# A streaming encoder layer on one core: attention in five steps, five heads' queries and keys by half products in front, small loads on another queue

## The chip, the cores and the metric

The kernel runs on one core of a Trainium2 chip. The metric is the device time of one execution in microseconds. The kernel before takes 2172.08 us, the median of three runs (2170.55 to 2174.25).

## What is computed

One layer with two parallel branches, for a prompt of 512 tokens and eight decode requests of 16 tokens each, so T = 640 columns in the kernel (NPT = 512 of them prompt). The width is 2048. Cut to what matters here:

```python
z = x @ w_in                      # q, k, v, forget logit and gate of FoX; GatedDeltaNet's inputs; merge gates
s = jnp.einsum('bqhd,bkhd->bhqk', q, k) * FOX_SCALE
bias = c_q - c_k                  # running sums of log forget, per head
p = jax.nn.softmax(jnp.where(visible, s + bias, -jnp.inf), axis=-1)
o_a = jnp.einsum('bhqk,bkhd->bqhd', p, v)
y_a = (o_a * jax.nn.silu(gate_a)) @ w_out_fox
...
h = (jax.nn.sigmoid(m_a) * y_a + jax.nn.sigmoid(m_b) * y_b) @ w_out
x1 = layer_norm(DEEPNORM_ALPHA * x + h, ln_g, ln_b)
x_out = x1 + jax.nn.sigmoid(x1 @ w_pl_gate) * rms_norm(p_l @ w_pl_proj, pl_norm_w)
```

FoX attention has eight heads of width 128. The prompt attends to itself; the decode tokens attend to caches of 512 keys and values per request (`kc`, `vc`) and to themselves.

## The kernel before

The activations lie transposed in SBUF, 128 channels by 640 tokens. A *column* is a projection onto 128 output channels: over 16 blocks of the width, every product is made of three matmuls of the halves of its operands (high by high, low by high, high by low), for two halves of 320 tokens. `column` (L396 and L397 in the rows, in its helper) makes 96 matmuls of 320 columns. `pair` (L474) makes two columns at once by seven half products, 168 matmuls in place of 192. The weights come from DRAM in tiles `wr` of 512 KB, issued by SP, are split into a high part `wh` by ACT (L329) and a low part `wl` by DVE (L335).

The phases follow one another: `front` (first columns, values, gates and the pairs), `phase_fox` (attention between the matmuls of plain columns, then a projection), `phase_gdn` (the other branch), `tail`. The order of the work is set when the program is built: every loop over dense matmuls calls `tick`, which lets *lanes* of generators emit their next piece. A generator yields how many ticks it wants to wait, and a model clock (`clock`, `busy`, `wrote`) keeps it from being resumed before its operands are likely to be there. What comes out is a fixed list of instructions for each engine; at run time only semaphores hold an engine back.

The queries and keys of head 0 and of the heads in `APART` (2, 3, 5, 6) are made by `front`, the latter as pairs, stored in a DRAM buffer `qkd`, and loaded again by SP in `phase_fox`. Heads 1, 4 and 7 get theirs from plain columns inside `phase_fox` (six columns), with three merge columns (`mcol`) beside them.

Attention is driven by `fox_all`. For each head `fox_in` loads what is small: the forget sums spread over the partitions (`nb` for the prompt, `nbd` for decode), the gate `sg`, the values `vn`; it also fills `qpad`, a padded copy of the decode queries, on GpSimd. Then four query blocks i = 0 to 3 go through `fox_step`, a pipeline over the list `flow`: `scores` (matmuls `s<-k,q` L754 for i = 0, `s<-kh,qh` and two more for the others at L388 to L390; three operations on DVE, the exponential on ACT), `softmax2` (a reciprocal and a scaling on DVE, L655 and L656), the transposes with the copy to `pT` (L726, L729), and the weighted sum `s<-pT,vn` (L742), which DVE multiplies by the gate into `og`. Within one call of `fox_step` the order before is: transposes of one block, `softmax2` of a later one, weighted sum of an earlier one; the new block's scores come after the call.

The decode tokens have a generator of their own, `fox_dec`: sixteen matmuls against the cached keys (`s<-kc,qpad`, L773), a softmax over `xd`, four transposes into `ppad` and one into `pn` (L793, L799; ACT's copies L795, L801), the weighted sum with `vc`. `fox_out` stores the head.

Each DMA of SP signals one of eight semaphores in turn (DMAHW0 to 7), and a transfer is issued when the one eight before it has landed; GpSimd's transfers have a set of their own (DMASW).

Of the kernel before, what the change touches and what calls it, by code (L numbers as in the profile page):

```python
# [52 lines left out]
class Kernel:  # L53
# [9 lines left out]
    APART = 2, 3, 5, 6  # L63
    NG = 8
    PAIR0, PAIRS = 6, NG + 2 + FRONT // 2 + len(APART)
    BETWEEN = 3, 6
# [6 lines left out]
    def __init__(self, tc, ins, outs):  # L73
        self.clock, self.busy, self.wrote, self.paced = 0.0, [0.0, 0.0, 0.0], {}, False
        self.tc, self.nc, self.i, self.o = tc, tc.nc, ins, outs
        self.lanes, self.every = [], 2
# [4 lines left out]
    def saw(self, ins):  # L81


        if ins.engine not in ENGINES or not ins.outs or not hasattr(ins.outs[0], "ap"):
            return
# [22 lines left out]
    def watch(self, gen):  # L108
# [7 lines left out]
        return abs(n), t + (0.25 if n > 0 else -1.5)  # L116
# [513 lines left out]
    def load_v(self, h):  # L630

        self.vn[h] = self.zt([P, 5, P], "vn", 2)
        self.nc.sync.dma_start(out=self.vn[h], in_=self.vd[:, :, h * P:(h + 1) * P].rearrange("t p d -> p t d"))

    def load_bias(self, h):
        nb = self.zt([P, T], "nb", 2)
        self.nc.sync.dma_start(out=nb, in_=bcast(self.rd[h], T, P))
        nbd = self.zt([P, NPT], "nbd", 2)
        self.nc.sync.dma_start(out=nbd, in_=bass.AP(self.sfd.tensor, self.sfd[h * 8].offset,
# [3 lines left out]
    def softmax1(self, xs, n):  # L643
# [3 lines left out]
        nm = self.zt([P, 1], "nm", 6)  # L647
        nc.vector.reduce_max(out=nm, in_=xs[:, 0:n], axis=AX.X, negate=True)
        sm = self.zt([P, 1], "sm", 6)
# [9 lines left out]
    def fox_in(self, h, q):  # L659

        nc = self.nc
        if h == 0:
            self.load_bias(0)
        self.sg[h] = self.zt([P, T], "sg", 2)
        nc.sync.dma_start(out=self.sg[h], in_=self.sgf[h])
        self.load_v(h)
        if h == 0:
            for j in range(4):
                self.load_kv(0, "k", j)

# [12 lines left out]

    def fox_all(self):


        flow = [None] * 4
        for h in range(H):
            while h not in self.heads or self.heads[h][2] > self.now or min(self.outdone, self.decdone) < h - 2:
                if any(flow):  # L690
                    self.fox_step(flow)
                yield 2
            q, k, _ = self.heads.pop(h)
            self.fox_in(h, q)
# [23 lines left out]
    def fox_step(self, flow):  # L718

        nc = self.nc  # L720
        spread = weigh = None
        if flow[1]:
            h, i, (xs, _) = flow[1]
# [7 lines left out]
        if flow[0]:  # L731
            h, i, (xs, sm) = flow[0]
# [1741 lines left out]
```

## Time and profile before

| | |
|---|---|
| median of three runs | 2172.08 us |
| the profiled execution | 2173.18 us |
| its span | 2171.3 us |
| granted TensorE clock, mean | 0.999 |
| attention stage, first scores to last weighted sum | 739.53 to 941.35 us |
| plain dense work ahead of it in the same phase, from | 721.92 us |

The span is the time between the first and the last instruction of the profiled execution; 1.9 us lie around it. Every row of the profile has an engine, a line of the kernel, an operation with its tiles (result<-operands), a count and times; a window's row has one group for each engine, busy time and count, then the granted clock, the busy share of the DMA engines and the rate. SPq is SP's queue: its rows are issues of transfers, not the transfers. TensorE's busy time in a row includes overlap, since matmuls are pipelined, so start times say more than durations.

### The profile page before, as it was taken

What the parts mean: (1) busy time and instruction counts of PE and PEld (TensorE: products, weight loads), DVE (VectorE), ACT (ScalarE), POOL (GpSimd) and SP (SyncE); (2) the same over time, 40 slices, a digit from 0 to 9 for tenths busy, and PEclk for the clock granted to TensorE, in tenths of its full rate; (3) what the DMA queues carried; (4) which work ended last, traced back from release to release, by engine and by line L of the source; (5) the groups of instructions that cost most, each with busy time, mean ns of one, the idle gap of its engine ahead of it and who ended that gap; (6) DMA issues with size and microseconds to landing.
All of it is one profiled execution on the core that took longest, in us unless ns stands there. A gap on an engine that the chain in (4) does not pass through costs nothing.

```text
span 2171.3 us, 41951 instructions
## 1 busy us (share of the span) xinstructions
PE 2149.0 (99%) x15438; PEld 2082.3 (96%) x15438; DVE 1566.0 (72%) x3207; ACT 1007.3 (46%) x2213; POOL 401.9 (19%) x596
## 2 busy tenths in 40 slices
PE   9999999999999999999999999999999999999998
PEld 7799999999999998899999999999999999999998
DVE  5877776767776565566478677766757787789987
ACT  4344443443444343353655566655443343354544
POOL 0022233323330101002334333332000000021100
PEclk9999999999999999999999999999999999999999
DMA  6356656666554899869978778878567656673465
GB/s 235 101 184 202 189 182 199 198 199 194 184 180 158 276 325 344 314 199 291 241 179 199 180 188 194 189 182 248 161 229 260 209 171 202 201 276 122 153 227 173
DMA packets 240670, 452.65 MB, mean 208 GB/s; under 512 B 38920, under 2 KB 122504, under 8 KB 240464
## 3 DMA queue, kind: packets, MB, share of 16 engines
q1 hardware_dynamic: 224912, 421.64, 59.5%
q0 software_dynamic: 15552, 28.32, 8.0%
q8 instruction: 122, 2.00, 0.4%
q14 instruction: 84, 0.69, 0.1%
HBM read 353.48 MB, written 96.38 MB: 207 GB/s over the span
## 4 chain that ended last, share of the span: by engine, by line
PE 91%; DVE 3%; DMA 3%; ACT 1%; SPq 0%; issue 0%; POOL 0%; ACTq 0%; DVEq 0%; POOLq 0%
PE g L474 44%; PE g L396 18%; PE g L397 18%; PE g L440 2%; PE s L974 1%; PE s L742 1%; PE s L813 1%; PE s L773 1%; DMA ws138b<-ws 0%; PE s L440 0%; PE s L1168 0%; DMA nb<-rd 0%; DVE sx L1006 0%; DVE sx L1004 0%; PE s L726 0%
## 5 line engine op out<-in xcount | busy, mean ns | idle before, releaser
L329 ACT CAST wh<-wr 128x512 fp32r<-128x512 f32 x624 | 381.2, 619 | 288.7 <-PE g L474 109.5
L335 DVE TENSOR_TENSOR wl<-wr,wh 128x512 fp32r<-128x512 f32 x516 | 358.3, 708 | 183.5 <-ACT wh L329 173.7
L474 PE MATMUL g<-xh,wh 128*128 128x320 f32 (+1 forms) x1296 | 402.9, 311 | 2.7 <-ACT m L1278 1.6
L474 PE MATMUL g<-xl,wh 128*128 128x320 f32 (+1 forms) x1296 | 401.2, 310 | 0.6 <-DVE xl L371 0.6
L474 PE MATMUL g<-xh,wl 128*128 128x320 f32 (+1 forms) x1296 | 401.4, 310 | 0.0
L396 PE MATMUL g<-xh,wh 128*128 128x320 f32 (+1 forms) x960 | 313.0, 326 | 0.7 <-ACT wh L329 0.7
L396 PE MATMUL g<-xh,wl 128*128 128x320 f32 (+1 forms) x960 | 297.1, 309 | 0.8 <-DMA wl<-in_w 0.7
L396 PE MATMUL g<-xl,wh 128*128 128x320 f32 (+1 forms) x960 | 297.2, 310 | 0.4 <-DVE xl L371 0.4
L397 PE MATMUL g<-xh,wh 128*128 128x320 f32 x960 | 297.3, 310 | 0.0
L397 PE MATMUL g<-xl,wh 128*128 128x320 f32 x960 | 297.0, 309 | 0.0
L397 PE MATMUL g<-xh,wl 128*128 128x320 f32 x960 | 296.7, 309 | 0.0
L474 PEld LDWEIGHTS g<-xh,wh 128*128 128x128 f32 x1296 | 243.9, 188 | 4.3 <-ACT m L1278 2.1
L474 PEld LDWEIGHTS g<-xl,wh 128*128 128x128 f32 x1296 | 243.7, 188 | 1.1 <-DVE xl L371 1.1
L474 PEld LDWEIGHTS g<-xh,wl 128*128 128x128 f32 x1296 | 244.1, 188 | 0.0
L474 PE MATMUL g<-t,wh 128*128 128x320 f32 (+1 forms) x1088 | 241.4, 310 | 0.0
L335 DVE TENSOR_TENSOR wl<-sr,wh 128x512 fp32r<-128x512 f32 x200 | 147.9, 759 | 98.6 <-ACT wh L329 97.6
L295 POOL TENSOR_TENSOR ws<-ws 128x171 f32<-128x171 f32 (+2 forms) x152 | 116.7, 768 | 541.5 <-DMA ws<-in_w 535.7
L396 PEld LDWEIGHTS g<-xh,wh 128*128 128x128 f32 x960 | 180.9, 188 | 11.9 <-issue 7.1
L474 PEld LDWEIGHTS g<-t,wh 128*128 128x128 f32 x1088 | 181.9, 188 | 0.6 <-issue 0.3
L396 PEld LDWEIGHTS g<-xh,wl 128*128 128x128 f32 x960 | 180.6, 188 | 1.4 <-DMA wl<-in_w 1.0
L397 PEld LDWEIGHTS g<-xh,wh 128*128 128x128 f32 x960 | 181.0, 189 | 0.9
L396 PEld LDWEIGHTS g<-xl,wh 128*128 128x128 f32 x960 | 180.9, 188 | 1.0 <-DVE xl L371 1.0
(440 smaller groups left out, 4148.8 us busy)
## 6 DMA issues: line engine op xcount, KB each, us to landing
wr<-in_w SPq DMA_DIRECT2D x252, 512.0 KB
wl<-in_w POOLq DMA_DIRECT2D x108, 256.0 KB, 5.8
kc<-in_kc SPq DMA_DIRECT2D x32, 512.0 KB
vc<-in_vc SPq DMA_DIRECT2D x32, 512.0 KB
sr<-in_w SPq DMA_DIRECT2D x25, 512.0 KB
ws<-in_w SPq DMA_DIRECT2D x96, 128.0 KB
sb<-in_w SPq DMA_DIRECT2D x80, 128.0 KB
md<-m SPq DMA_DIRECT2D x32, 320.0 KB
```

Of the source, the lines that this page charges most:

```text
L295: nc.gpsimd.tensor_tensor(out=o, in0=x, in1=y, op=op)
L329: nc.scalar.copy(out=hi, in_=src)
L335: nc.vector.tensor_tensor(out=lo, in0=src, in1=hi.bitcast(F32), op=ALU.subtract)
L396: nc.tensor.matmul(ps[0], whl[w], xhl[o][:, a], start=(first and x == 0), stop=(last and x == 2))
L397: nc.tensor.matmul(ps[1], whl[w], xhl[o][:, b], start=(first and x == 0), stop=(last and x == 2))
L440: nc.tensor.matmul(ps, x[:, sl], w, start=(s == 0 and n == 0), stop=(s == 15 and n == 2))
L474: nc.tensor.matmul(ps, a[:, w], b, start=(k == 0 and n == 0 and not more), stop=(k == last and n == 2), skip_group_check=True)
L742: nc.tensor.matmul(ops[:, 0:P], vn[:, kb, :], pT[:, kb * P:(kb + 1) * P], start=(kb == 0), stop=(kb == i))
L773: nc.tensor.matmul(s1[32 * j:32 * j + 32, :], self.qpad[:, 2 * j + par, :], kc[:, (j % 2) * NPT:(j % 2 + 1) * NPT], start=(par == 0), stop ...
L813: nc.tensor.matmul(od[32 * j:32 * j + 32, 0:P], self.ppad[:, c, 2 * j + par, :], vc[:, o:o + P], start=False, stop=(par == 1 and c == 3), ...
L974: nc.tensor.matmul(pp[:, o:o + 256].rearrange("p (a b) -> p a b", a=2), kq[:, 0, x], kq[:, :, x], start=True, stop=True)
```

## The change

- `APART` becomes 1, 2, 3, 6, 7: five heads in `front` by pairs. Only heads 4 and 5 have plain columns in `phase_fox` (`JOBS`), with the three merge columns; their q and k go through `qkd` too. All heads load q and k by a new function `load_qk`.
- `fox_all` loads q, k, nb, nbd and the four key caches of head 0 first, then q and k of head 1 and the four value caches of head 0; `sg` and `vn` of head 0 come with `fox_in`, behind these. For head 0 SP issues them; for later heads GpSimd issues nb, nbd, sg and vn, and q and k from head 2 on. A head starts when the model clock is 21.5 past the start of the one before (`PACE`); lanes may be resumed at every tick (`every`) and without lead (`lead`); transfers no longer count in the model clock.
- `fox_step` takes the new block as an argument and has a list of five: transposes, weighted sum, the new scores, then `softmax2` of the block before. The score tiles are one per block (`xs0` to `xs3`) instead of three in turn.
- The decode part's transposes move into `fox_dec2`, a lane of its own, with `pn` ahead of the four transposes; `xd` has two buffers.
- `weight_sums` does its thirteenth slice in `front`. The tiles of the projection (`pr`) are loaded inside a merge column. In the evacuation of the projection three tiles come from `kc` at once and three from `vc` later; squares use one `kc` tile and one more tile, `og`.

TensorE has 24 dense matmuls fewer by this, GpSimd issues 40 transfers more, SP fewer.

The diff, without buffer counts, `lead`, the DRAM buffers of `qkd` and the host's ordering of the weights:

```diff
@@ -60,10 +60,11 @@
     FRONT = 32 - 3 - 7
-    APART = 2, 3, 5, 6
     NG = 8
+    APART = 1, 2, 3, 6, 7
     PAIR0, PAIRS = 6, NG + 2 + FRONT // 2 + len(APART)
-    BETWEEN = 3, 6
+    PACE = 21.5
+    JOBS = 4, 5, None, None
     FILL = 0, 0, 1, 0, 1, 0, 1, 4
@@ -81,7 +82,7 @@
-        if ins.engine not in ENGINES or not ins.outs or not hasattr(ins.outs[0], "ap"):
+        if ins.engine not in ENGINES or "DMA" in type(ins).__name__ or not ins.outs or not hasattr(ins.outs[0], "ap"):
             return
@@ -630,13 +631,13 @@
         self.vn[h] = self.zt([P, 5, P], "vn", 2)
-        self.nc.sync.dma_start(out=self.vn[h], in_=self.vd[:, :, h * P:(h + 1) * P].rearrange("t p d -> p t d"))
+        (self.nc.gpsimd if h else self.nc.sync).dma_start(out=self.vn[h], in_=self.vd[:, :, h * P:(h + 1) * P].rearrange("t p d -> p t d"))
...
         nb = self.zt([P, T], "nb", 2)
-        self.nc.sync.dma_start(out=nb, in_=bcast(self.rd[h], T, P))
+        (self.nc.gpsimd if h else self.nc.sync).dma_start(out=nb, in_=bcast(self.rd[h], T, P))
         nbd = self.zt([P, NPT], "nbd", 2)
-        self.nc.sync.dma_start(out=nbd, in_=bass.AP(self.sfd.tensor, self.sfd[h * 8].offset,
+        (self.nc.gpsimd if h else self.nc.sync).dma_start(out=nbd, in_=bass.AP(self.sfd.tensor, self.sfd[h * 8].offset,
                                                     [[NPT, 8], [0, 16], [1, NPT]]))
@@ -659,15 +660,9 @@
         nc = self.nc
-        if h == 0:
-            self.load_bias(0)
         self.sg[h] = self.zt([P, T], "sg", 2)
-        nc.sync.dma_start(out=self.sg[h], in_=self.sgf[h])
+        (nc.gpsimd if h else nc.sync).dma_start(out=self.sg[h], in_=self.sgf[h])
         self.load_v(h)
-        if h == 0:
-            for j in range(4):
-                self.load_kv(0, "k", j)
-
         for par in range(2):
@@ -681,26 +676,35 @@
+    def load_qk(self, h):
+        qk = []
+        for c in range(2):
+            qk.append(self.zt([P, T], "qk"[c], 2))
+            (self.nc.gpsimd if h > 1 else self.nc.sync).dma_start(out=qk[c], in_=self.qkd[h, c])
+        self.heads[h] = *qk, self.clock + (7 if h else 5)
+
     def fox_all(self):
...
-        flow = [None] * 4
+        flow, begun = [None] * 5, 0.0
+        self.load_qk(0)
+        self.load_bias(0)
+        for j in range(4):
+            self.load_kv(0, "k", j)
+        self.load_qk(1)
+        for j in range(4):
+            self.load_kv(0, "v", j)
         for h in range(H):
-            while h not in self.heads or self.heads[h][2] > self.now or min(self.outdone, self.decdone) < h - 2:
+            while h not in self.heads or max(self.heads[h][2], begun + self.PACE) > self.clock or min(self.outdone, self.decdone) < h - 2:
                 if any(flow):
...
             q, k, _ = self.heads.pop(h)
+            begun = self.clock
             self.fox_in(h, q)
-            if h == 0:
-                yield 5
-                for j in range(4):
-                    self.load_kv(0, "v", j)
-                yield 4
             parts = None
             for i in range(4):
-                self.fox_step(flow)
-                flow[0] = h, i, self.scores(h, i, q, k, parts)
+                self.fox_step(flow, (h, i, q, k, parts))
                 if i == 0:
@@ -708,19 +712,21 @@
                 if i == 1 and h + 1 < H:
-                    while self.qkdone[1] < h - 1:
+                    while self.qkdone[1] < h - 1 or h + 1 not in self.kept:
                         yield 1
                     self.load_bias(h + 1)
+                    if h:
+                        self.load_qk(h + 1)
         while any(flow):
...
-    def fox_step(self, flow):
-
-        nc = self.nc
-        spread = weigh = None
-        if flow[1]:
-            h, i, (xs, _) = flow[1]
+    def fox_step(self, flow, new=None):
+
+        nc = self.nc
+        spread = ops = None
+        if flow[2]:
+            h, i, (xs, _) = flow[2]
             pt = self.sps()
@@ -728,22 +734,23 @@
             spread = h, i, pT
-        if flow[0]:
-            h, i, (xs, sm) = flow[0]
-            self.softmax2(xs, P * (i + 1), sm)
-            weigh = flow[0]
-        if flow[2]:
-            h, i, pT = flow[2]
-            if i == 0:
-                self.og = self.zt([P, T], "og", 2)
-            vn, sl = self.vn[h], slice(i * P, (i + 1) * P)
+        if flow[3]:
+            h, i, pT = flow[3]
+            vn = self.vn[h]
             ops = self.sps()
...
                 nc.tensor.matmul(ops[:, 0:P], vn[:, kb, :], pT[:, kb * P:(kb + 1) * P], start=(kb == 0), stop=(kb == i))
+            if i == 0:
+                self.og = self.zt([P, T], "og", 2)
+            sl = slice(i * P, (i + 1) * P)
             nc.vector.tensor_tensor(out=self.og[:, sl], in0=ops[:, 0:P], in1=self.sg[h][:, sl], op=ALU.mult)
...
                 self.outs["gens"].append(self.fox_out(h, self.sg[h], self.og))
-        flow[:] = None, weigh, spread, None
+        new = (*new[0:2], self.scores(*new)) if new else None
+        if flow[1]:
+            h, i, (xs, sm) = flow[1]
+            self.softmax2(xs, P * (i + 1), sm)
+        flow[:] = None, new, flow[1], spread, None
@@ -788,6 +795,14 @@
         yield -2
+        self.decs2["gens"].append(self.fox_dec2(h, xd))
+
+    def fox_dec2(self, h, xd):
+        nc = self.nc
+        pt = self.sps()
+        nc.tensor.transpose(pt[:, 0:P], xd[:, NPT:T], self.ident)
+        pn = self.zt([P, P], "sq", 2, "pn")
+        nc.scalar.copy(out=pn, in_=pt[:, 0:P])
         pt = self.dps()
@@ -795,11 +810,7 @@
                 in_=pt.rearrange("p (c j two x) -> p c j two x", c=4, two=2, x=16)[:, :, :, par, :])
-        pt = self.sps()
-        nc.tensor.transpose(pt[:, 0:P], xd[:, NPT:T], self.ident)
-        pn = self.zt([P, P], "sq", 2, "pn")
-        nc.scalar.copy(out=pn, in_=pt[:, 0:P])
-        yield 4
+        yield 2
         while self.outdone < h - 1:
@@ -1506,48 +1517,40 @@
         self.outdone = self.decdone = -1
-        self.heads, self.sg = {}, {}
+        self.heads, self.sg, self.kept = {}, {}, {0, *self.APART}
+        self.every, self.lead = 1, 0.0
         work["gens"].append(self.fox_all())
...
         self.vn = {}
-        ws = self.zt([P, 1024], "ws")
-        self.sums["gens"].append(self.weight_sums([ws[:, x:x + 256] for x in range(0, 1024, 256)], slice(12, 13),
-                                                  (9, 7, 5, 20)))
-        for h in range(H):
-            qk = []
-            if h in self.BETWEEN:
+        todo = deque((h, c) for h in self.JOBS for c in range(1 if h is None else 2))
+
+        def job():
+            h, c = todo.popleft()
+            if h is None:
                 self.mcol("eacc")
-            for c in range(2):
-                stored = (h, c) in self.qkd
-                if not stored:
-                    acc = self.column()[0]
-                self.until(lambda: min(self.qkdone) >= h - 2)
-                x = self.zt([P, T], "qk"[c], 2)
-                qk.append(x)
-                if stored:
-                    nc.sync.dma_start(out=x, in_=self.qkd[h, c])
-                    continue
-                for hf in range(2):
-                    sl = slice(hf * HALF, (hf + 1) * HALF)
-                    if c == 0:
-                        nc.scalar.mul(x[:, sl], acc[hf], FOX_SCALE)
-                    else:
-                        nc.scalar.copy(out=x[:, sl], in_=acc[hf])
-                if c:
-                    nc.sync.dma_start(out=self.o["fk"][h], in_=x)
-            self.heads[h] = *qk, self.now + (9 if stored else 1)
-        for _ in range(2 - len(self.BETWEEN)):
-            self.mcol("eacc")
+                return
+            acc = self.column()[0]
+            x = self.zt([P, T], "pr", 1, "qk")
+            for hf in range(2):
+                sl = slice(hf * HALF, (hf + 1) * HALF)
+                if c == 0:
+                    nc.scalar.mul(x[:, sl], acc[hf], FOX_SCALE)
+                else:
+                    nc.scalar.copy(out=x[:, sl], in_=acc[hf])
+            nc.sync.dma_start(out=self.qkd[h, c], in_=x)
+            if c:
+                nc.sync.dma_start(out=self.o["fk"][h], in_=x)
+                self.kept.add(h)
+        while todo:
+            job()
         op, pr = [], []
-        for k in range(2):
-            if k == 0:
-                self.until(lambda: not self.sums["gens"])
-            pr.append(self.zt([P, 1024], "ws", 1, "pr")[:, 0:T] if k == 0 else self.zt([P, T], "pr"))
-            nc.sync.dma_start(out=pr[k], in_=self.i["pT"][k])
-
         def after(s):
+            if s in (4, 6):
+                self.until(lambda: min(self.qkdone) >= 6)
+                pr.append(self.zt([P, T], "nb", 2, "pr") if s == 4 else self.zt([P, T], "pr"))
+                nc.sync.dma_start(out=pr[-1], in_=self.i["pT"][s // 2 - 2])
             if s in (12, 14):
@@ -1778,11 +1782,14 @@
-            self.until(lambda: self.decdone == 7 and not self.sums["gens"])
+            self.until(lambda: self.qkdone[1] == 7 and not self.sums["gens"])
             self.eacc = self.zt([P, T], "eacc")
-            tiles = [self.zt([P, 1024], *x, "e")[:, 0:T] for x in (("kc", 4), ("kc", 4), ("ws", 1), *[("vc", 4)] * 4)]
-            self.e_tiles, self.q_tiles = tiles[0:5], tiles[5:7]
+            tiles = [self.zt([P, 1024], "kc", 4, "e")[:, 0:T] for _ in range(4)]
+            self.e_tiles, self.q_tiles = tiles[0:3], [tiles[3], self.zt([P, T], "og", 2, "e")]
             self.esq = None
+        if n == 6:
+            self.until(lambda: self.decdone == 7)
+            self.e_tiles += [self.zt([P, 1024], "vc", 4, "e")[:, 0:T] for _ in range(3)]
         e = self.e_tiles[n % len(self.e_tiles)]
```

How the instructions move is shown at three places. The first is SP at the start of attention, behind the stores of the last pair; the names are those of the text above, and the brackets hold the semaphores waited for. Before:

```order
L269 DMA wr<-in_w 128x1024
L269 DMA wr<-in_w 128x1024 [waits DVE_49]
L637 DMA nb<-rd 128x640 [waits DMAHW4_49]
L639 DMA nbd<-sfd 128x1x512
L665 DMA sg<-sgf_169 128x640
L633 DMA vn<-vd 128x5x128
L627 DMA kc<-in_kc 128x1024 [waits DMAHW0_49]
L627 DMA kc<-in_kc 128x1024 [waits DMAHW1_49]
L627 DMA kc<-in_kc 128x1024 [waits DMAHW2_49]
L627 DMA kc<-in_kc 128x1024 [waits DMAHW3_49]
L269 DMA wr<-in_w 128x1024 [waits DMAHW4_49,DVE_49]
L627 DMA vc<-in_vc 128x1024 [waits DMAHW5_49]
```

After:

```order
L628 DMA kc<-in_kc 128x1024 [waits DMAHW3_49]
L628 DMA kc<-in_kc 128x1024 x3
L683 DMA q<-qkd_187 128x640 [waits DMAHW7_49]
L683 DMA k<-qkd_188 128x640 [waits DMAHW0_49]
L628 DMA vc<-in_vc 128x1024 [waits DMAHW1_49]
L628 DMA vc<-in_vc 128x1024 [waits DMAHW2_49]
L628 DMA vc<-in_vc 128x1024 [waits DMAHW3_49]
L628 DMA vc<-in_vc 128x1024 [waits DMAHW4_49]
L270 DMA wr<-in_w 128x1024 [waits DMAHW5_49]
L664 DMA sg<-sgf_169 128x640 [waits DMAHW6_49]
L634 DMA vn<-vd 128x5x128 [waits DMAHW7_49]
```

`sg` and `vn` stood ahead of the caches `kc` and `vc`; now they stand behind them, behind q and k of head 1 (the second pair of L683) and behind a weight tile. The wait on DMAHW7 of `vn` is for the slot of the second load of q.

The second place is ACT in the decode part of a head in the middle of attention, around the copies to `ppad` and `pn`. Before:

```order
L650 ACTIVATE xs,sm<-xs,nm 128x256 [waits DVE_49]
L329 CAST wh<-wr 128x512 [waits PE_49]
L795 COPY ppad<-s 128x16x16 [waits PE_49]
L795 COPY ppad<-s 128x16x16
L801 COPY pn<-s 128x128 [waits PE_49]
L729 COPY pT<-s 128x128 [waits PE_49,Activation_49]
L650 ACTIVATE xs,sm<-xs,nm 128x384 [waits DVE_49]
```

After:

```order
L651 ACTIVATE xs_9320,sm<-xs_9320,nm 128x384 [waits DVE_49]
L330 CAST wh<-wr 128x512 [waits PE_49]
L805 COPY pn<-s 128x128 [waits PE_49]
L810 COPY ppad<-s 128x16x16 [waits PE_49]
L810 COPY ppad<-s 128x16x16
L735 COPY pT<-s 128x256 [waits PE_49,Activation_49]
L651 ACTIVATE xs_9381,sm<-xs_9381,nm 128x512 [waits DVE_49]
```

The copy to `pn` now comes ahead of the two copies to `ppad`, each of which frees a PSUM bank.

The third place is DVE in a step of the pipeline, an earlier head's: the reciprocal and the scaling of `softmax2`, the gate product into `og`, and the three operations of new scores. Before:

```order
L655 RECIPROCAL sm<-sm 128x1
L656 TENSOR_SCALAR xs<-xs,sm 128x128 [waits DVE_49]
L743 TENSOR_TENSOR og<-s,sg 128x128 [waits PE_49]
L759 SCALAR_TENSOR_TENSOR xs<-nb,colT,s 128x256 [waits PE_49]
L761 TENSOR_TENSOR xs<-xs,cb 128x128 [waits DVE_49]
L648 TENSOR_REDUCE nm<-xs 128x1 [waits DVE_49]
```

After:

```order
L746 TENSOR_TENSOR og<-s,sg 128x128 [waits PE_49]
L766 SCALAR_TENSOR_TENSOR xs_8971<-nb,colT,s 128x256 [waits PE_49]
L768 TENSOR_TENSOR xs_8971<-xs_8971,cb 128x128 [waits DVE_49]
L649 TENSOR_REDUCE nm<-xs_8971 128x1 [waits DVE_49]
L656 RECIPROCAL sm<-sm 128x1
L657 TENSOR_SCALAR xs_8863<-xs_8863,sm 128x128 [waits DVE_49]
```

The scaling of a block has moved from ahead of the weighted sum and the new scores to behind them.

More of the change, by code (lines that the diff above doesn't have):

```diff
@@ L75, in __init__ @@
         self.tc, self.nc, self.i, self.o = tc, tc.nc, ins, outs
-        self.lanes, self.every = [], 2
+        self.lanes, self.every, self.lead = [], 2, 1.5
         self.banks, self.read, self.nbanks = [], {}, 3
@@ L115, in watch @@
         t = max([y for x, y in zip(b, self.busy) if x != y] + [0.0])
-        return abs(n), t + (0.25 if n > 0 else -1.5)
+        return abs(n), t + (0.25 if n > 0 else -self.lead)
     def lane(self, dry=False):
@@ L646, in softmax1 @@
         nc = self.nc
-        nm = self.zt([P, 1], "nm", 6)
+        nm = self.zt([P, 1], "nm", 4)
         nc.vector.reduce_max(out=nm, in_=xs[:, 0:n], axis=AX.X, negate=True)
-        sm = self.zt([P, 1], "sm", 6)
+        sm = self.zt([P, 1], "sm", 5)
         nc.scalar.activation(xs[:, 0:n], xs[:, 0:n], AF.Exp, bias=nm, accum_out=sm)
@@ L757, in scores @@
             self.mm3(s[:, 0:w], [x[:, (i - 1) * P:i * P] for x in qp], kp, slice(0, w), True, True)
-        xs = self.zt([P, NPT], "xs", 3)
+        xs = self.zt([P, w], f"xs{i}")
         nc.vector.scalar_tensor_tensor(out=xs[:, 0:w], in0=nb[:, 0:w], scalar=self.colT[:, i, h:h + 1],
@@ L776, in fox_dec @@
         nc.tensor.matmul(s2[:, 0:P], q[:, NPT:T], k[:, NPT:T], start=True, stop=True)
-        xd = self.zt([P, T], "xd")
+        xd = self.zt([P, T], "xd", 2)
         cq = self.colT[:, 4, h:h + 1]
@@ L1239, in run @@
         self.sgd = self.sgf[H:]
-        self.qkd = {(h, i): dr([P, T], F32, name=f"qkd{h}{i}") for h in (0, *self.APART) for i in range(2)}
+        self.qkd = {(h, i): dr([P, T], F32, name=f"qkd{h}{i}") for h in range(H) for i in range(2)}
         self.vd = dr([5, P, 1024], F32, name="vd")
@@ L1247, in run @@
         self.nm = 0
-        self.outs, self.decs = self.lane(), self.lane()
+        self.outs, self.decs2, self.decs = self.lane(), self.lane(), self.lane()
         work, conv, self.ends = self.lane(), self.lane(True), self.lane()
@@ L1467, in weights @@
             ws = self.zt([P, T], "nb", 1, "ws"), self.spare[1]
-            yield from self.weight_sums([t[:, x:x + 256] for t in ws for x in (0, 256)], slice(0, 12), (6, 4, 2))
+            yield from self.weight_sums([t[:, x:x + 256] for t in ws for x in (0, 256)], slice(0, 13), (6, 4, 2))
         self.sums["gens"].append(weights())
@@ L1563, in phase_fox @@
         nc.sync.dma_start(out=self.sqd, in_=self.eacc)
+        self.every, self.lead = 2, 1.5
     def mcol(self, tag, **kw):
@@ L2383, in _layout @@
     rest = iter(m[nf:nf + 3])
-    for h in range(1, H):
-        bl += [next(rest) for _ in range(h in Kernel.BETWEEN)]
-        if h not in Kernel.APART:
-            bl += [bq[h], bk[h]]
+    for h in Kernel.JOBS:
+        bl += [next(rest)] if h is None else [bq[h], bk[h]]
     bl += rest
```

## Prediction

> **What bounds the kernel now.** The page comes first: busy shares, then the chain that ended last.
>
> ```profile
> span 2171.3 us, 41951 instructions
> PE 2149.0 (99%) x15438; PEld 2082.3 (96%) x15438; DVE 1566.0 (72%) x3207; ACT 1007.3 (46%) x2213; POOL 401.9 (19%) x596
> PE 91%; DVE 3%; DMA 3%; ACT 1%; SPq 0%; issue 0%; POOL 0%; ACTq 0%; DVEq 0%; POOLq 0%
> PE g L474 44%; PE g L396 18%; PE g L397 18%; PE g L440 2%; PE s L974 1%; PE s L742 1%; PE s L813 1%; PE s L773 1%; DMA ws138b<-ws 0%; PE s L440 0%; PE s L1168 0%; DMA nb<-rd 0%; DVE sx L1006 0%; DVE sx L1004 0%; PE s L726 0%
> ```
>
> TensorE is busy for 99% of the span, and 80% of the chain is the dense projections (L474, L396, L397). So an edit counts by what it does to TensorE: matmuls removed, or time in which it stands still. The table of windows shows both, for a pure stretch of half products and for the part that the change rewrites: its lead-in of plain dense work, then attention.
>
> ```profile
> core 0: us, PE busy (x) PEld busy (x) DVE busy (x) ACT busy (x) POOL busy (x), PEclk, DMA share, GB/s
> 120.00:320.00 200.00, 200.00 (x1364) 200.00 (x1364) 153.95 (x203) 85.72 (x155) 58.86 (x60) 1.00 0.59 187
> 721.92:739.53 17.61, 17.61 (x122) 17.61 (x121) 5.44 (x10) 4.35 (x9) 2.09 (x4) 1.00 0.76 245
> 739.53:941.35 201.82, 198.83 (x1831) 180.59 (x1829) 123.91 (x299) 80.37 (x215) 16.28 (x30) 1.00 0.87 312
> ```
>
> A dense matmul of 320 columns costs 200.00/1364 = 0.147 us. In attention TensorE stands still for 201.82 − 198.83 = 2.99 us; that is all that smoother attention can win there. The DMA columns matter more: 0.59 busy among the half products, 0.87 through attention. The list of waits from 735 to 990 says what those 2.99 us wait for, in its three largest rows:
>
> ```profile
> PE s L754 <- ACT pn L801: 0.8, 1, 0.8
> PE s L388 <- ACT pn L801: 0.8, 1, 0.8
> PE s L388 <- DVE xd L780: 0.7, 2, 0.5
> ```
>
> Last, the start of attention, where the change reorders the loads: TensorE's timeline, then SP's.
>
> ```profile
> 721.92 0.31 PE L396 MATMUL g<-xh,wh 128*128 128x320 f32 x1
> 739.53 0.38 PE L754 MATMUL s<-k,q 128*128 128x128 f32 x2
> 749.41 0.31 PE L397 MATMUL g<-xh,wl 128*128 128x320 f32 x1
> 749.64 1.92 PE L773 MATMUL s<-kc,qpad 128*32 128x512 f32 x16
> 752.04 0.39 PE L742 MATMUL s<-pT,vn 128*128 128x128 f32 x2
> ```
>
> ```profile
> 726.66 0.32 SPq L1529 DMA_DIRECT2D q<-qkd  x1
> 730.14 1.26 SPq L633 DMA_DIRECT2D vn<-vd  x1
> 731.44 4.67 SPq L627 DMA_DIRECT2D kc<-in_kc  x4
> 737.62 3.33 SPq L627 DMA_DIRECT2D vc<-in_vc  x4
> 749.59 0.60 SPq L639 DMA_DIRECT2D nbd<-sfd  x1
> ```
>
> I call 721.92 T0: the first matmul of the plain column with which this stage begins. q can be loaded only at T0 + 4.7, behind the stores of the last pair. Between T0 and the first scores stand 17.6 us, 120 dense matmuls, and until the first weighted sum, at T0 + 30.1, TensorE waits for nothing: this lead hides the loads.
>
> **The change part by part.**
>
> *One more head by half products.* Five heads instead of four are done in pairs: 168 matmuls for two columns where a plain pair takes 192. 24 × 0.147 = 3.5 us less, on the path, since TensorE is full on both sides. The fifth head's stores go to DRAM beside pairs whose DMA share is 0.59; I cost them nothing, and at most the landing of one 320 KB tile if the queue were full there.
>
> *The order inside a step, and pn ahead of the four transposes of xd.* ACT frees pn's bank two copies earlier and weighted sums stand ahead of new scores, so the two waits on pn should go. The gain lies between 0 and 2.99 us; I take 3.0, since the rows name just the edges that are cut.
>
> *More switches.* By the program's order the stage's dense work falls into 63 blocks instead of 49, as attention is called at every tick. A switch costs the step from 749.41 to 749.64, 0.23 us, less the usual 0.147: 0.08. 14 × 0.08 = 1.1 us.
>
> *DVE's order.* The second half of a softmax (L656) now stands behind the next scores' three operations. Where they wait for their matmul, the normalisation waits too, and behind it the transposes that read it two steps on. With five steps in flight I take 0.5 us in all; between 0 and 4, half a microsecond for each of eight heads, the size of the longest wait that DVE causes above.
>
> *Head 0's loads.* This term decides the sum. Before, sg and vn (v of head 0) went out ahead of kc and vc, the caches; now they stand behind q, k, nb, nbd, four kc, q and k of head 1, four vc and a weight tile. At the same time attention starts sooner: by the new order the first scores come after 42 dense matmuls instead of 120, and the first weighted sum, the first reader of vn, after 96, which with 3.5 us of small matmuls (2.4 of them the stretch 749.64 to 752.04) and four switches is T0 + 14.1 + 3.5 + 0.3 = T0 + 17.9.
>
> When does vn land? SP waits for the landing of the transfer eight earlier before it issues the next, which dates landings:
>
> ```profile
> 739.35 0.33 SPq L627 DMA_DIRECT2D vc<-in_vc  x1
> 740.63 0.33 SPq L627 DMA_DIRECT2D vc<-in_vc  x1
> SPq L627 <- DMA kc<-in_kc: 0.9, 1, 0.9
> SPq L627 <- DMA vn<-vd: 0.7, 1, 0.7
> ```
>
> vn, issued at 730.14, let the third vc go only at 739.35, 9.2 us later; each kc after it took 1.28 us more. So what SP issues lands in its order, one after another. The rate and the sizes:
>
> ```profile
> 726.66:749.59 22.93, 22.93 (x158) 22.78 (x157) 8.86 (x21) 6.22 (x15) 2.09 (x4) 1.00 0.96 338
> 741.00:747.00 6.00, 6.00 (x43) 5.99 (x42) 3.80 (x9) 3.20 (x9) 0.00 (x0) 1.00 1.02 408
> kc<-in_kc SPq DMA_DIRECT2D x32, 512.0 KB
> vn<-vd SPq DMA_DIRECT2D x8, 320.0 KB
> nbd<-sfd SPq DMA_DIRECT2D x8, 256.0 KB
> ```
>
> q, k, nb and sg have vn's 320 KB, a vc or weight tile kc's 512 KB. Before, from q up to the third vc go five small tiles (q, k, nb, sg, vn), nbd, and ten large ones (three weight tiles, four kc, three vc): 5 × 0.328 + 0.262 + 10 × 0.524 = 7.14 MB, landed at 749.59, when the next head's nbd could go out. After, up to and with vn: 7 × 0.328 (q, k, nb, q, k, sg, vn), nbd, and nine large ones are 7.28 MB, 0.14 MB or 0.3 us more. So vn lands at 749.9 = T0 + 28.0, and TensorE, which is there at T0 + 17.9, waits 10.1 us. Lower bound: all 7.28 MB at 408 GB/s from 726.66 is 17.8 us, T0 + 22.5, a wait of 4.6. Upper bound: GpSimd now issues nb, nbd, sg and vn of head 1 (1.25 MB) as soon as head 0's qpad is filled; before, that was here:
>
> ```profile
> 729.65 0.89 POOL L672 COPY qpad<-q 128x64 f32<-128x64 f32 x2 [1.73 <-DMA q<-qkd]
> wl<-in_w POOLq DMA_DIRECT2D x108, 256.0 KB, 5.8
> ```
>
> At T0 + 8.6 they are in the middle of it. If the engines take turns between the queues, they delay vn by 1.25/0.408 = 3.1 us, a wait of 13.2. The second row speaks for sharing: a GpSimd tile of 256 KB lands 5.8 us after its issue beside SP's stream, not in 0.6. [...] I take 11, near the value that the row of before gives (10.1), and on the side of the upper bound.
>
> [...]
>
> Loads of later heads keep their lead of a head's length, over 20 us for some 6 MB, 15 us at 408 GB/s; I cost the move to GpSimd nothing there, within the 0 to 4 above. Buffers renamed, the weight sum's last slice moved in front and e's tiles taken from other pools change no matmul; nothing for these.
>
> Sum, against the profiled execution's 2173.2 us (2171.3 span and 1.9 around it): −3.5 − 3.0 + 1.1 + 0.5 + 11.0 = +6.1, so 2179.3. That execution lies 1.1 above the median of 2172.08, so 2178.2: **2178**.
>
> **The rivals.** About 0.2%, 4.3 us, is what a measurement of this kernel tells from no change.
>
> *A: the loads are there in time, faster.* If the stores in front of q are done earlier, or vn doesn't queue behind the caches, the 11 us are gone: −3.5 − 3.0 + 1.1 = −5.4, and 2166.7. For it: before, TensorE met no wait for a load in this stretch, and the share of 0.96 leaves some room. Against it: landings 1.28 us apart at 408 GB/s, and even the lower bound leaves 4.6 us. It decides if vn lands by T0 + 18.
>
> *B: only about 5 us of wait.* The lower bound, 4.6, up to 9.2: −3.5 − 3.0 + 1.1 + 0.5 + 4.6 = −0.3 up to +4.3: 2172 to 2176, no change that can be told. For it: the mean of 338 GB/s holds a slow first stretch, which an order without the two early weight tiles may shorten. Against it: the same stores and the same first loads stand there.
>
> *C: steady waits, slower still.* Every head starts close behind the one before, and DVE, held by scores, delays xs for the transposes by 1 us a head, eight heads: +8 on top of the sum, 2186. For it: DMA is at 0.87 and one stage more per step waits on DVE. Against it: DVE is busy for 123.91 of 201.82 us, and each step has a dense block to hide in.
>
> **How the numbers follow.** The start's wait of 9.2 us or more 0.48, C 0.14 (slower together 0.62), B 0.24 (same), A 0.14 (faster). The forecast's own range is 2176 to 2183: a wait of 9.2 to 13.2, the pn gain kept or lost. C's end sets 2186; A at 2166.7 is where I stop, 2167.
>
> **What would show it.** In the profile after, right: a wait of TensorE on vn at the first weighted sum (L742 in the new order's line), one piece of 6 to 9 us behind smaller ones for k and kc, 11 in all before the first head's second step; no rows on pn; 24 dense matmuls fewer. A falls if any wait on vn is above 1 us; B is right if the waits there add up to 4 to 9; C shows as waits on xs or pT in every head. My prediction is wrong if TensorE meets the first weighted sum without a wait, or if later heads wait for q, k or sg, which I costed at nothing.

## The result, and the profile after

The changed kernel takes 2191.26 us, the median of four runs (2189.82 to 2191.89), beside 2173.12 us for the kernel before, now of four runs: a ratio of 1.0085, with a 95% interval of 1.0072 to 1.0097. It is slower by 18 us, where 6 were forecast. The page of the changed kernel, its span, busy times and chain:

```profile
span 2189.0 us, 42003 instructions
PE 2150.2 (98%) x15414; PEld 2080.5 (95%) x15414; DVE 1575.4 (72%) x3222; ACT 1013.5 (46%) x2219; POOL 433.6 (20%) x636
PE 50%; DVE 3%; DMA 2%; ACT 1%; issue 0%; SPq 0%; POOL 0%; ACTq 0%; POOLq 0%; DVEq 0%
```

TensorE has 24 matmuls fewer and is busy 1.2 us longer, in a span 17.7 us longer. The list of what it waits for between 744 and 1000 us, the attention stage and the projection, in its largest rows (in total, times, longest):

```profile
PE s L742 <- DMA vn<-vd: 8.5, 1, 8.5
PE s L761 <- POOL qpad L667: 2.8, 1, 2.8
PE g L397 <- ACT m L1575: 1.6, 1, 1.6
PE s L780 <- DMA kc<-in_kc: 1.4, 1, 1.4
PE g L397 <- DVE e L1795: 1.0, 1, 1.0
PE s L389 <- ACT kh L675: 0.9, 1, 0.9
```

No row on pn is among them, and none on xs or pT. The start in TensorE's timeline:

```profile
747.38 0.31 PE L397 MATMUL g<-xh,wh 128*128 128x320 f32 x1
756.50 0.46 PE L761 MATMUL s<-k,q 128*128 128x128 f32 x2 [2.79 <-POOL qpad L667]
761.44 0.38 PE L389 MATMUL s<-kh,qh 128*128 128x256 f32 x1 [0.94 <-ACT kh L675]
762.16 0.38 PE L390 MATMUL s<-kl,qh 128*128 128x256 f32 x1 [0.34 <-DVE kl L676]
771.00 1.05 PE L780 MATMUL s<-kc,qpad 128*32 128x512 f32 x4 [1.45 <-DMA kc<-in_kc]
781.21 0.80 PE L742 MATMUL s<-pT,vn 128*128 128x128 f32 x2 [8.52 <-DMA vn<-vd]
```

T0 is 747.38 here. 2.79 + 0.94 + 0.34 + 1.45 + 8.52 = 14.0 us of waits before the first weighted sum, which comes at T0 + 33.8. SP's queue over the same time, from its timeline:

```profile
752.18 0.32 SPq L683 DMA_DIRECT2D q<-qkd  x1
758.73 6.21 SPq L628 DMA_DIRECT2D vc<-in_vc  x4
770.97 0.33 SPq L664 DMA_DIRECT2D sg<-sgf  x1
771.98 0.38 SPq L634 DMA_DIRECT2D vn<-vd  x1
```

vn is not even issued before T0 + 24.6. Last, the windows: the long wait, what follows it, and two stretches in which GpSimd's transfers run beside SP's.

```profile
core 0: us, PE busy (x) PEld busy (x) DVE busy (x) ACT busy (x) POOL busy (x), PEclk, DMA share, GB/s
772.69:781.20 8.51, 0.00 (x0) 0.00 (x0) 1.53 (x4) 1.18 (x3) 0.00 (x0) 0.65 1.05 392
781.20:785.55 4.35, 4.34 (x15) 4.05 (x16) 2.42 (x6) 0.40 (x1) 1.18 (x3) 0.50 1.00 395
762.18:764.18 2.00, 2.00 (x14) 2.00 (x15) 1.90 (x6) 0.18 (x1) 0.00 (x0) 1.00 1.09 271
764.18:766.18 2.00, 2.00 (x15) 1.99 (x14) 1.06 (x3) 1.20 (x4) 0.00 (x0) 1.00 1.02 243
```

The granted clock is 0.50 for the 4.35 us behind the wait, in which TensorE gets through 15 matmuls: 2.2 us lost. And in these two stretches, while GpSimd's tiles are under way, the DMA engines are fully busy (1.09, 1.02) but move 271 and 243 GB/s, not 408.

The table has the stages of the profiled executions by start times in TensorE's timelines, from T0 up to the first matmul on `re`, behind the projection (977.14 before, 992.92 after). "Rest" is the stage less 0.1467 us for each dense matmul: small matmuls, waits and lost clock. "Half" counts the pieces of 3.41 us at half clock within the stage. The ratio is from all runs, the other columns from one execution each: that of e1 and e5 was the fastest of their runs, that of e2, e3, e4, e7 and e9 the slowest.

| kernel | ratio to before (interval) | first weighted sum, T0 + | stage | rest | half |
|---|---|---|---|---|---|
| before | 1 | 30.1 | 255.2 (1140 dense) | 88.0 | 0 |
| after | 1.0085 (1.0072 to 1.0097) | 33.8 | 245.5 (948 dense) | 106.5 | 3 |
| e1, sg and vn ahead | 1.0046 (1.0031 to 1.0061) | 24.3 | 238.8 | 99.7 | 2 |
| e2, head 1 by SP | 1.0042 (1.0028 to 1.0057) | 28.0 | 240.8 | 101.7 | 3 |
| e3, late start | 1.0109 (1.0094 to 1.0124) | 48.4 | 256.8 | 117.7 | 7 |
| e4, pace 19 | 1.0054 (1.0037 to 1.0072) | 34.6 | 245.6 | 106.5 | 5 |
| e5, loads as read | 1.0027 (1.0018 to 1.0036) | 24.4 | 234.3 | 95.3 | 2 |
| e6, e5 at pace 19 | 1.0045 (1.0030 to 1.0060) | 24.5 | 240.4 | 101.3 | 2 |
| e7, pn last | 1.0088 (1.0071 to 1.0105) | 32.8 | 248.2 | 109.2 | 5 |
| e8, softmax first | 1.0147 (1.0130 to 1.0163) | 34.1 | 247.0 (942 dense) | 108.8 | 4 |
| e9, before, five pairs | 1.0072 (1.0059 to 1.0085) | 30.1 | 247.8 | 108.8 | 4 |
| e10, e5 at even pace | 1.0050 (1.0034 to 1.0067) | 22.5 | 242.4 | 103.3 | 3 |
| e11, wait filled | 1.0072 (1.0059 to 1.0085) | 33.2 | 244.6 | 105.5 | 1 |
| e12, start only | 1.0062 (1.0049 to 1.0074) | 23.1 | 240.7 | 101.6 | 3 |

The stage has 192 dense matmuls fewer, 28.2 us, and is shorter by 9.7: its rest has grown by 18.5.

### The profile page after: what moved, and what is told of

Read it like the earlier page. It is cut to its first block, busy times and chain, and to the rows that moved or that the text cites. A ratio compares the mean times of both kernels' runs of the same rounds, so it can differ in the third digit from the quotient of the medians.

```text
span 2189.0 us, 42003 instructions
## 1 busy us (share of the span) xinstructions
PE 2150.2 (98%) x15414; PEld 2080.5 (95%) x15414; DVE 1575.4 (72%) x3222; ACT 1013.5 (46%) x2219; POOL 433.6 (20%) x636
## 4 chain that ended last, share of the span: by engine, by line
PE 50%; DVE 3%; DMA 2%; ACT 1%; issue 0%; SPq 0%; POOL 0%; ACTq 0%; POOLq 0%; DVEq 0%
PE g L475 16%; PE g L397 15%; PE g L398 14%; PE s L985 1%; DVE sx L1015 1%; DVE sx L1017 1%; DMA ws138b<-ws 0%; PE s L1179 0%; DVE cy L891 0%; DMA wr<-ws105S 0%; DMA lanes<-ld 0%; DMA wl<-in_w 0%; PE s L1207 0%; PE s L1212 0%; DMA wr<-in_w 0%
## 5 line engine op out<-in xcount | busy, mean ns | idle before, releaser
L398 PE MATMUL g<-xh,wh 128*128 128x320 f32 x928 | 287.9, 310 | 0.0
L398 PE MATMUL g<-xl,wh 128*128 128x320 f32 x928 | 287.3, 310 | 0.0
L398 PE MATMUL g<-xh,wl 128*128 128x320 f32 x928 | 287.0, 309 | 0.0
L475 PEld LDWEIGHTS g<-xh,wl 128*128 128x128 f32 x1328 | 250.1, 188 | 0.4 <-DVE wl L336 0.4
L336 DVE TENSOR_TENSOR wl<-sr,wh 128x512 fp32r<-128x512 f32 x208 | 156.2, 770 | 102.2 <-ACT wh L330 101.2
L296 POOL TENSOR_TENSOR ws<-ws 128x171 f32<-128x171 f32 (+2 forms) x140 | 109.6, 783 | 507.3 <-DMA ws<-in_w 502.4
L330 ACT CAST wh<-sr 128x512 fp32r<-128x512 f32 x208 | 124.8, 618 | 132.9 <-PE g L475 104.8
```

The source lines that it names most:

```text
L296: nc.gpsimd.tensor_tensor(out=o, in0=x, in1=y, op=op)
L330: nc.scalar.copy(out=hi, in_=src)
L336: nc.vector.tensor_tensor(out=lo, in0=src, in1=hi.bitcast(F32), op=ALU.subtract)
L398: nc.tensor.matmul(ps[1], whl[w], xhl[o][:, b], start=(first and x == 0), stop=(last and x == 2))
L475: nc.tensor.matmul(ps, a[:, w], b, start=(k == 0 and n == 0 and not more), stop=(k == last and n == 2), skip_group_check=True)
```

## The experiments

My theory after the result: the place of sg and vn in SP's order, behind the caches, makes TensorE wait at the first weighted sum, and that wait halves the clock (0.50 over the 4.35 us behind it). The rivals: GpSimd's transfers of head 1 hold vn back, not its place; the start is simply too early; heads this close are what costs.

**e1 and e2: place, or turns.** e1 takes the loads of sg and vn out of `fox_in` into a function of their own, `load_sv`, and calls it for head 0 ahead of head 1's q and k:

```diff
             self.load_kv(0, "k", j)
+        self.load_sv(0)
         self.load_qk(1)
```

> After, with sg and vn of head 0 issued by SP right behind the four kc, ahead of q and k of head 1 and the four vc; TensorE's order is the same. Theory 1 (the place in SP's order sets when vn lands): vn lands some 1.6 us behind the last kc, the wait on vn falls from 8.5 to under 1.5 us, the clock stays at full speed through the start, 2191.3 - 8 - 2 = 2181, within 2179 to 2183. Theory 2 (turns with GpSimd's four transfers hold vn back, not its place): the wait stays above 5 us and the time above 2187.

e2 changes `self.nc.gpsimd if h else self.nc.sync` to `self.nc.gpsimd if h > 1 else self.nc.sync` for nb, nbd, sg and vn.

> After, with nb, nbd, sg and vn of head 1 issued by SP as head 0's are, so that GpSimd starts no transfer in the first 20 us of attention; TensorE's order is the same. Theory 1 (vn's place behind the caches): as after, 2191, or up to 1 us less. Theory 2 (turns with GpSimd's 1.25 MB): 3.1 us less wait for kc and vn together, 14.0 to about 11; the clock still drops, since more than 5 us of it stay in one piece: 2188.

TensorE's largest waits at the start of e1, then of e2:

```profile
PE s L767 <- POOL qpad L672: 2.3, 1, 2.3
PE s L809 <- DVE xd L657: 2.3, 1, 2.3
PE s L748 <- DMA vn<-vd: 0.8, 1, 0.8
```

```profile
PE s L742 <- DMA vn<-vd: 5.9, 1, 5.9
PE s L761 <- POOL qpad L667: 2.4, 1, 2.4
```

Both causes are real: each of the two edits takes off about half of the loss by the ratios, e1 8.5 and e2 9.3 of 18.5 us; in e2's profile the stage is only 4.7 us shorter. In e1 the wait on vn is 0.8 us; 1.0046 is 2183, the upper end of what the place should give. Its clock did not stay at full speed, as had been expected: the two pieces at half clock stand behind the waits of 2.3 us, the second from 783.34 to 786.75 us, at 0.50. e2's 1.0042 is 2182, 6 us less than the turns were priced at. In e2 the first weighted sum comes at T0 + 28.0, which is the figure that the prediction worked out for SP's bytes alone; with GpSimd's transfers it is T0 + 33.8. So GpSimd's transfers cost 5.8 us, not 3.1: 1.25 MB at the 243 to 271 GB/s of the windows above, 4.6 to 5.1 us, explains most of it. The rest, up to 1.2 us, stays unexplained. Two windows of e2 show what the low rate goes with:

```profile
756.18:758.18 2.00, 1.70 (x12) 1.73 (x13) 0.00 (x0) 0.00 (x0) 0.00 (x0) 1.00 1.00 248
762.18:764.18 2.00, 2.00 (x16) 2.00 (x15) 1.76 (x6) 0.49 (x2) 0.00 (x0) 1.00 1.02 406
```

Without GpSimd's transfers the stretch from 762.18 has its 406 GB/s. But in the first window, behind SP's issue of head 0's q, k, nb and nbd, the rate is as low, and no transfer of GpSimd runs. So the low rate seems to belong to some of the small tiles, whoever issues them, and not to the turns. The kernel before shows it too: 238 GB/s from 732.66 to 734.66, at a DMA share of 0.84, behind the same loads. Which of the tiles is slow was not tried.

**e3: the late start.** `self.clock + (7 if h else 5)` becomes `... else 16.4)`.

> After, with head 0 held back by the model clock so that its scores come after 126 dense matmuls instead of 42; attention then ends at dense matmul 840 of the stage instead of 798. Theory 1 (the early start has no data yet): the start's 14 us of waits and the 2 us of half clock go, and the waits in the projection, 3.5 us, grow by 1 to 3: 2177, within 2175 to 2180. Rival (the early start pays for itself, a later one is paid back at the end of attention): 2186 or more.

It missed, by 20 us. The largest wait of TensorE, and what ACT, which owes it `kh`, waited for:

```profile
PE s L389 <- ACT kh L675: 14.8, 1, 14.8
```

```profile
779.64 0.62 ACT L330 CAST wh<-wr 128x512 fp32r<-128x512 f32 x1 [17.81 <-DMA wr<-in_w]
```

With more dense work ahead of the scores, TensorE needs weights earlier than vn, and the weight tiles stand behind the same caches. ACT's cast of such a tile waits 17.8 us, and in ACT's order the exponential and `kh` of head 0 stand behind it. So a later start alone does not cure it: what is ahead in the queue is too much, whoever reads first. The kernel before had two weight tiles right behind q and k.

**e5 and e12: the order in which loads are read.** Both issue sg and vn ahead of kc, and vc and head 1's q and k behind head 0's second block, and keep head 1's small loads on SP. e5 also lets head 0 start after 66 dense matmuls; e12 keeps 42, so all heads stand as in after.

```diff
+        self.load_sv(0)
         for j in range(4):
             self.load_kv(0, "k", j)
-        self.load_qk(1)
-        for j in range(4):
-            self.load_kv(0, "v", j)
...
-                    if h:
-                        self.load_qk(h + 1)
+                    if h == 0:
+                        for j in range(4):
+                            self.load_kv(0, "v", j)
+                    self.load_qk(h + 1)
```

> After, with head 0's loads in the order in which they are read (q, k, nb, nbd, sg, vn, kc, then weight tiles, and vc and head 1's q and k only behind head 0's second block), head 1's small loads by SP as well, and the first scores after 66 dense matmuls instead of 42; attention ends at dense matmul 702 of the stage instead of 798. Theory (order and volume of the ring in front of the first readers): the start's waits fall from 14.0 to under 3 us, the clock never drops, 2 us, and the projection's waits fall from 3.5 to about 2: 2191.3 - 11.5 - 2 - 1.5 = 2176, within 2174 to 2179. Rival (what is taken away at the start comes back at a later load, as in the late start): 2184 or more, with a wait above 5 us at another tile.

> After, with only head 0's loads put in the order in which they are read and head 1's small ones with SP; all heads start at the same dense matmul as in after (42 to 618), attention ends at 798. Theory (start waits 14 and clock 2, the rest of the loss in the projection, 3.5, stays): 2191.3 - 11 to 13 - 2 = 2177.5, within 2176 to 2180, with the projection's waits unchanged at 3.5. Rival (another tile takes over at the start, as with the late start): 2184 or more.

TensorE's largest waits in the stage in e5, then in e12:

```profile
PE s L737 <- DVE xs L657: 4.6, 3, 2.5
PE s L808 <- DVE xd L657: 1.6, 1, 1.6
```

```profile
PE s L785 <- DMA kc<-in_kc: 3.0, 2, 2.0
PE s L766 <- POOL qpad L672: 2.4, 1, 2.4
PE g L397 <- ACT m L1580: 1.6, 1, 1.6
PE g L397 <- DVE e L1800: 1.1, 1, 1.1
```

In e5 all waits for transfers are gone, and 12 of the 18 us (1.0027 is 5.9 us above before; after is 18.5 by its ratio). That is 2179, the upper end of what was expected; the clock did drop, for two pieces. The waits left stand where heads 6 and 7 follow at 42 dense matmuls' distance, and at the first transposes of head 0. e12 missed: 1.0062 is 2186.6, in the rival's range. Its start has 3 us of waits instead of 14, but head 1's caches are now 3.0 us late, the projection's waits are as they were, and three pieces of half clock lie in the stage, two of them behind waits of 2 to 2.4 us. Between e12 and e5 only the start differs, 42 or 66 dense matmuls, and with it the place of all heads: with the loads in this order the later start is worth about 7.6 us by the ratios. So the early start is part of the loss too.

**e4, e6 and e10: the pace.** PACE 19 on after (e4) and on e5 (e6), 20.5 on e5 with head 0 after 54 dense matmuls (e10).

> After, with PACE 19 instead of 21.5: the last head ends at dense matmul 654 of the stage, ahead of the projection, which begins at 672, instead of 798. Theory (ACT and DVE free the projection's banks late because head 7's softmax stands in front of them): the 3.5 us of waits in the projection go and the start stays as it is, 2188. Rival C of the prediction (heads this close wait in every step): 1 us more for each of seven heads, 2195 or more.

> The kernel with loads in the order in which they are read, and PACE 19: attention ends at dense matmul 654 of the stage, ahead of the projection at 672. Theory: the projection's waits are gone as well, 2 us less than without the pace: 2174; with 24 dense matmuls fewer than the kernel before this could be 1 to 2 us below it, 2172. Rival C (heads this close wait in each step): 2180 or more.

> The kernel with loads in the order in which they are read, first scores after 54 dense matmuls and PACE 20.5: heads start every 60 to 78 dense matmuls, none bunched at the end as in the run before it without the pace, and attention ends at 672, where the projection begins. Theory: the waits on xs at the end (3.7 us) and in the projection are gone, those for kc and vc of the run with pace 19 are at most 1 to 2 us: 2176, or 2174 if none. Rival (the transfers of a head don't fit into its pace): 3 us or more of waits for kc, vc or k in the first four heads, 2180 or more.

The largest waits of e4, then of e10:

```profile
PE s L742 <- DMA vn<-vd: 6.7, 1, 6.7
PE s L761 <- issue: 3.4, 1, 3.4
PE s L761 <- DMA k<-qkd: 2.4, 1, 2.4
PE s L780 <- DMA kc<-in_kc: 2.1, 2, 1.9
```

```profile
PE s L766 <- DMA k<-qkd: 4.6, 1, 4.6
PE s L785 <- DMA kc<-in_kc: 3.2, 3, 2.3
```

e4 comes out 3 us below what was expected (1.0054 is 2185). In all three, attention ends ahead of the projection and no row on m or e is left: the theory of the projection's waits holds. In after they are 1.6 on m and 1.0 and 0.4 on e, 3.1 in all; the 3.5 of the expectations holds one more of 0.4, head 7's own on og, which falls between them. ACT's timeline in after, just ahead of the largest:

```profile
943.11 0.61 ACT L651 ACTIVATE xs<-xs,nm 128x384 f32<-128x384 f32 x1 [2.17 <-DVE nm L649]
943.73 0.74 ACT L1575 ACTIVATE m<-g 128x320 f32<-128x320 f32 x2
```

ACT evacuates a bank (L1575, in other places L1794) only behind head 7's exponential, which waits for DVE's work on the scores. But what closer heads save there they lose on transfers: k of a middle head, stored by a plain column and loaded again, comes 2.4 us late in e4 and 4.6 in e10; vc, k and kc together 6.1 in e6. e6 and e10 come out 0.18 and 0.23% above e5, with intervals that just overlap. The rival is right for them, mostly by transfers, not by DVE; but the late k of e10 is head 5's, behind the first four heads that the rival named.

**e7 and e8: the order of the steps.** e7 puts pn's transpose and copy behind the copies to ppad again; e8 puts `softmax2` ahead of the weighted sum again.

> After, with the transpose and the copy of pn behind the four transposes of xd and their copies again, as before the change; all else as after. Theory (ACT's place for pn freed the bank late): waits on pn come back, 1.6 to 2.9 us in the whole stage, 2193. Rival (the new order of the steps removed these waits, not pn's place): none comes back, 2191.

> After, with the second half of the softmax ahead of the weighted sum and of the new scores again; the planner then closes attention at dense matmul 726 of the stage instead of 798. Theory (DVE's order costs nothing in the steady heads): the start stays as it is, only the projection's waits shrink by 1 to 2 us, 2190. Rival C of the prediction (scores in front of the softmax hold DVE back by half a microsecond or more a head): 4 us or more less, 2187 or below, with fewer waits on xs and pT in the middle of the stage.

e7's time can't be told from after's (1.0088 and 1.0085), but its list of waits has the row again that the move had removed:

```profile
PE s L389 <- ACT pn L812: 1.7, 5, 0.4
```

e8 answers nothing: its stage is as long as after's (247.0 and 245.5), while the order of the next phase, which the model clock plans, came out otherwise and made that 12.9 us longer (522.6 between `re` and the last `s<-kqs`, 509.8 in after). That DVE's order costs little in the steady heads rests on after's own list, without a row on xs or pT.

**e9: five pairs on the kernel before.** `APART = 2, 3, 4, 6, 7`, `BETWEEN = 4, 6`, nothing else.

> The kernel before, with one part of the change alone: five heads by pairs (2, 3, 4, 6, 7; heads 1 and 5 stay plain columns, merge columns ahead of heads 4 and 6), its own loads, steps and queues. The first scores still come after 120 dense matmuls, and attention ends at 720 of the stage. Theory (the pair's 3.5 us are real, and the loss of the change lies in its start): no wait at the first weighted sum, waits of the order of 3 us in the projection, since it begins at 672; 2173 - 3.5 + 3 = 2172.5, within 2169 to 2175. Rival (attention among 600 dense matmuls instead of 780 is what costs, wherever it starts): waits in many steps, 2180 or more.

```profile
PE s L742 <- DMA vn<-vd: 3.3, 1, 3.3
PE s L388 <- DVE xd L780: 2.4, 3, 1.8
PE s L388 <- ACT pn L801: 1.9, 3, 1.0
PE s L754 <- ACT k L1536: 1.9, 1, 1.9
PE s L754 <- ACT pn L801: 1.7, 2, 1.1
PE g L396 <- ACT ph L1556: 1.6, 1, 1.6
```

The rival is right. The start is as before, without a wait, and 0.72% are lost all the same, to waits in many steps, the largest on a late head's vn, and to four pieces of half clock: with 600 dense matmuls around attention instead of 780, the old steps are no longer covered. e5, with as many dense matmuls in the stage and all the rest of the change, its loads put in order, loses 0.45% less; how much of that is the new order of the steps no run separates.

**e11: the wait filled.** Thirty matmuls of the constant tile in front of head 0's first weighted sum, into its bank.

> After, with thirty 128x128 matmuls of a constant tile, some 6.6 us, in front of head 0's first weighted sum, into the bank that this sum then overwrites: TensorE works while it waits for vn. All else as after. Theory (the piece of 8.5 us without work halves the clock, which costs the 4 us behind it half their speed): the clock stays at full speed from 772 to 786, and the time falls by about 2 us although thirty matmuls are added: 2189. Rival (the clock costs nothing on the path, since the transfers set it): 2191 to 2192.

```profile
771.00:781.20 10.20, 8.43 (x71) 8.11 (x70) 2.33 (x6) 1.18 (x3) 0.06 (x1) 1.00 1.04 394
781.20:784.63 3.43, 3.43 (x15) 3.43 (x14) 2.03 (x5) 1.90 (x5) 2.30 (x4) 0.50 1.00 392
```

The clock stays at 1.00 through the wait, and yet one piece at half clock follows, 0.50 over the 3.43 us of the second row, behind the 1.8 us that were left of the wait. The ratio is lower than after's by 0.13%, about as expected, but the intervals overlap: the direction is right, the size is not settled by this run.

No version beats the kernel before; e5 comes nearest.

## Why the prediction was wrong

The direction and the place were right, and so were the signs that the prediction named: one piece of 8.5 us on vn behind smaller waits, no row on pn. The size was not, and it fell outside the range. The term of the loads, the largest, was 3 us too small; with that alone the forecast would have been 2181, still within 2176 to 2183. What took the time out of the range are costs that the prediction put at nothing: the clock, the waits in the projection and a remainder behind it, 7.8 us together. The terms, forecast and measured:

- *Five heads by pairs*, −3.5: 747.38 − 721.92 = 25.5 for 168 matmuls more, 28.2 for 192 fewer: −2.7. The kernels with the same front have T0 between 745.65 and 747.78, so −3.5 is inside that spread.
- *"I take 11" for head 0's loads*: 14.0, of which 1.3 are waits for kh and kl and not for loads. SP's own order gave T0 + 28.0, as e2's profile has it, though the agreement to a tenth is luck; the step that failed is the price of GpSimd's transfers, 1.25 MB at 408 GB/s, of which besides I took only a part. They cost 5.8 us, in stretches in which the DMA engines were full (1.09 and 1.02) at 271 and 243 GB/s. TensorE itself would have been there at T0 + 33.8 − 14.0 = 19.8, not 17.9, or the wait would have been longer. That the engines take turns between the queues was a supposition of mine, and no run shows it; what e2 shows is that SP's stream is ahead by 5.8 us without GpSimd's transfers. The upper end was still too low.
- *The clock*: no term; 2.2 us in this stage, at 0.50 over the 4.35 us behind the wait on vn. The profile of before could have warned me: it has such a place, in the next phase. The row of its waits, then the windows of that wait and of the stretch behind it:

```profile
PE s L1196 <- DVE uu L1074: 1.9, 1, 1.9
```

```profile
1444.62:1448.03 3.41, 1.49 (x11) 1.22 (x10) 3.28 (x8) 0.00 (x0) 0.68 (x1) 1.00 0.82 174
1448.03:1451.44 3.41, 3.41 (x15) 3.41 (x14) 3.31 (x10) 2.16 (x4) 0.61 (x1) 0.50 1.09 290
```

No window of the prediction covers this place.

- *The projection*: no term; 3.1 us on m and e. I counted that attention ends at dense matmul 798 and that the projection begins at 672, and did not ask who evacuates the projection's banks meanwhile.
- *The order inside a step*, −3.0: the old 2.9 us are gone, waits of 0.5 (at head 1's matmuls on kc; the profile names no cause) and 0.4 (og) came: −2.1. e7 gives 1.7 to the place of pn.
- *Switches*, +1.1, and *DVE's order*, +0.5: what is left of the stage is about +1.3 for both. No run separates them.
- Behind the projection, +2.5 with TensorE's work in the same order, a term that I had at nothing. In e1, with the same order there, it is +1.0. Why it differs stays open.

−2.7 + 14.0 + 2.2 + 3.1 − 2.1 + 1.3 + 2.5 = 18.3, by which the last dense matmul moved (2162.99 to 2181.26). The sum closes because 1.3 and 2.5 are remainders, not measured causes.

Of the rivals, A and B fell: the wait was above even the upper bound. C did not come in after, but its cousin by transfers did in e4, e6 and e10. What I had as a gain of the pairs alone, 3.5 us, could not be had alone either: e9.

## What to carry to other kernels

When loads change their order on a queue, add up, for every first reader, weight tiles included, all bytes in front of it, and count what another queue sends meanwhile at the rate that such tiles reach in the trace (243 to 271 GB/s here), not at the best one (408). A later start does not help while the tiles that the waiting time itself needs stand in the same queue (e3, with 14.8 us of wait on kh); it does once the loads stand in the order in which they are read (e5 beside e12, 7.6 us by the ratios). And where work slides into the next phase, look for the engine that serves both in one order: it pays there what was saved (3.1 us on m and e in after).

## What the runs showed of the hardware

The granted clock of TensorE fell to 0.50 in pieces of 3.41 us. In after the two stretches at half clock ahead of the last few microseconds begin at 775.31 and 1300.96 us and last 10.24 and 3.41 us, three pieces and one; their starts lie 525.65 us apart, which is 154 such pieces. Cut into these pieces from about 100 us to the last few microseconds, the trace of before has 603 of them at full clock, that of after 605. In before one of them was followed by a piece at half clock: the one from 1444.62 us, with TensorE busy for 1.49 us of 3.41. In after there were two: from 771.90, busy for 0.79 us, and from 1297.55, busy for 2.55. No drop came in after behind the pieces from 754.83 and 942.56, busy for 1.74 and 1.78 us, nor in before behind that from 1280.78, which was busy for 2.55 as well; so the busy time of a piece alone does not settle it.

In three of these runs the wait itself was shorter than 3.41 us. In before TensorE waited 1.92 us on uu, up to 1447.48 us and within one piece, and the next piece was at half clock. In e1 the piece from 779.93 us, busy for 1.06 us, holds the wait of 2.3 us on xd, and that from 783.34 was at 0.50. In e11 it was 1.8 us on vn. In after the same wait on uu, 1.94 us up to 1465.78, fell on two pieces, busy for 2.45 and 2.43 us, and that of 2.79 us on qpad, up to 756.50, on two that were busy for 2.29 and 1.74 us: the clock stayed at 1.00. In these five places a wait of 1.8 to 2.8 us cost a piece at half clock where it lay within one piece, and nothing where it fell on two. Such a piece costs an estimated 1.7 us, half of its 3.41.
